# A matmul with batch normalization: one more raw block and one more y buffer

## The chip, the cores and the metric

The kernel runs on one core of a Trainium2 chip. The metric is the time of one execution on the device, in microseconds (us). Three runs of the kernel before gave 206.24, 206.34 and 206.34 us; their median is 206.34 us. A separate execution was profiled.

## The reference

```python
y = np.matmul(x, weight)                      # x: 16 x 512 x 1024, weight: 1024 x 768, float32
mean = np.mean(y, axis=(0, 1), keepdims=True)
var = np.var(y, axis=(0, 1), keepdims=True)
y_norm = (y - mean) / np.sqrt(var + eps)
return (gamma * y_norm + beta).astype(np.float32)
```

There are 8192 rows (16 x 512) and 768 columns. Each column needs its mean and variance over all rows before its first output can be written.

## The kernel before, in words

**Tiling.** The 768 columns are six tiles of 128, called nt = 0 to 5. The 8192 rows are 16 chunks c of 512. x and weight are loaded and cast to bf16 by GpSimd's DMA queue (L386, L402); VectorE turns x so that the depth of 1024 stands on the partitions (L424, L431). x stays on the chip, turned, to the end.

**Tiles 0 and 1** are computed while x arrives, with rows on the partitions (L506). ScalarE squares each block (L655), VectorE adds it to `sum1` (L658), and VectorE or GpSimd adds the squares to `sum2` or `sum3` (L662). When the last chunk but two is in, `merge` (L791) and `more` (L796) fold the accumulators into one row of sums and one row of squares, in a tile of their own, `tot`; TensorE sums those over the partitions (L867). The last two chunks take another path (L810). The output is formed by `rows_out` (L926): a product on VectorE (L933), an addition on VectorE or GpSimd (L938), a store (L942).

**Tiles 2 to 5** are computed with columns on the partitions (L571), chunk after chunk: tile 2 over chunks 4 to 15 from about 104 us on, then tiles 3, 4 and 5 (chunks 0 to 3 of all were done early, L571 too). Statistics are taken on VectorE (L707), or for tile 2 on ScalarE (L716, L720), and the block is kept in bf16 (L711) in a y buffer of 1024 rows, that is, two chunks. `finish_tasks` (L964) makes scale and shift of a tile. Then each y buffer has to be scaled, turned back to rows, widened to float32 and stored, in one of these ways:

- `col_block` (L1187) in mode `xact`, tiles 2 and 3: a scaling on ScalarE (tile 2) or VectorE (tile 3, L1022), a DMA turn on SyncE's queue (L1216), a conversion on ScalarE (L1228), a store (L1198).
- `col_block` in mode `pe`, tile 4: a scaling on VectorE, a turn on TensorE between the products of tile 5 (L1040), a conversion on ScalarE (L1206), a store.
- a **raw block**: the unscaled buffer is turned by DMA ahead of time, into another y buffer (`raw_turn`, L1095, its DMA is L1102). Once scale and shift are known, `raw_spread` (L1123) lays them out along the rows (L1137 to L1154, with seven small copies on GpSimd or ScalarE, L1141, and a copy into PSUM, L1154), and `raw_block` (L1162) makes a product on VectorE (L1170), an addition on GpSimd (L1174) and a store (L1178). `RAW` lists the blocks by their first chunk: chunks 0 and 2 of tile 2, chunk 0 of tile 3, chunks 0, 2 and 4 of tile 4.
- `held_block` (L1236): the last block of tile 4, held back and stored (L1251) while the statistics of tile 5 are made.

Tile 5 comes last: its statistics end with L1304, scale and shift with L1320, and then its blocks are scaled (L1344), turned on TensorE (L1040), converted (L1357) and stored (L1360). In the text below tile nt = 3 is "the fourth tile" and nt = 4 "the fifth".

**Plain chunks.** For some chunks ScalarE or VectorE copies the turned x into a plain layout `x_pl` (`part_chunk`, L524, L543); for the chunks 12 to 15 this is done just before tile 4, by whichever engine the planner picks.

**The order of the work** is made while the program is built: every step is a `Task` with a priority, the engines that could do it with an estimated duration, and what it waits for. `arrange` (L122) takes the tasks one by one, by engine free times, buffers (`Pool`, `Space`), the DMA lanes (`Wires`) and priority, and so writes a fixed order for each engine. A change to one number can move instructions of other steps.

**Buffers.** Product results have 8 PSUM banks. There are `YB` = 28 y buffers of 2 KB per partition, shared by kept blocks, turned raw blocks and one plain chunk part; and a ring of 24 KB per partition (`RING`, `Space`) for loaded x, later for turned blocks (2 KB) and float32 output blocks (4 KB). SyncE's queue (SPq) issues all stores and turns in order; each waits for the landing of the eighth one before it at the latest.

**Gamma and beta** are loaded by `load_affine` (L406), twelve transfers of 128 values on SyncE's queue, one pair per tile.

Of the kernel before, what the change touches and what calls it, by code (L numbers as in the profile page):

```python
# [227 lines left out]
def kernel(  # L228
# [9 lines left out]
    nc = tc.nc  # L238
    f32 = mybir.dt.float32
# [8 lines left out]
    P = 128  # L248
    NT = N // P
# [3 lines left out]
    C = M // CH  # L253
# [9 lines left out]
    EARLY = 4  # L263
    SHORT = 2
    GA = 2
    NA = GA * P
    GY = 2
    PAD = 50
    HELD = 1
    ASTAT = {2:tuple(range(4,16))}  # L270
    RC = C - 2
    XT, YB, SQ = C - EARLY, 28, 3
    ADDED = (0,6,16,28,40)
    PARTED, LATE, SINGLE = (4,5,7,8,9,10), (12,13,14,15), (2,3,6)
    MODE = {2:'xact',3:'xact',4:('pe',)*8}
    MODE = {nt: m if isinstance(m, tuple) else (m,) * (C // GY) for nt, m in MODE.items()}
    RAW, RAWADD, RAWDUE = {2:(0,2),3:(0,),4:(0,2,4)}, {2:'POOL',3:'POOL',4:'POOL'}, {2:14.0,3:8.0,4:8.0}
    RING = 3 * CH // 32 * KQ // 2
    ENG = {"ACT": nc.scalar, "DVE": nc.vector, "POOL": nc.gpsimd, "SP": nc.sync}

# [3 lines left out]
    singles = ctx.enter_context(tc.tile_pool(name="singles", bufs=1))  # L284
# [7 lines left out]
    def seq(bi):  # L292

        ins = bi.ins
        prev = last.get(ins.engine)
        if prev is not None:
            tc.add_manual_dep(
                ins, prev,
                mybir.DependencyInfo(mybir.DependencyClass.NoSync, mybir.DependencyReason.DATA),
                reason="order",  # L300
            )
        last[ins.engine] = ins.name
        return bi

    gamma_sb = singles.tile([P, NT], f32)
# [10 lines left out]
    ones = singles.tile([P, 1], f32)  # L316
    seq(nc.vector.memset(ones, 1.0 / (RC * CH)))
    ident32 = singles.tile([P, P], f32)
    sum1 = singles.tile([P, 2 * NA], f32)
    sum2 = singles.tile([P, 2 * NA], f32)  # L320
    sum3 = singles.tile([P, 2 * NA], f32)
    for acc in (sum1, sum2, sum3):
        seq(nc.vector.memset(acc, 0.0))
    tot = singles.tile([P, 2, NA], f32)
    stats = singles.tile([P, (NT - GA) * C + PAD, 6], f32)
    fin = singles.tile([P, 9 + 6 * len(PIECES)], f32)
    psums = {nt: singles.tile([P, 2, C], f32, name=f"psums{nt}") for nt in ASTAT}
    sums = {nt: singles.tile([P, 4 + 6 * C], f32, name=f"sums{nt}") for nt in ASTAT}
    for nt in ASTAT:
        seq(nc.vector.memset(sums[nt][:, 1:2], float(len(ASTAT[nt]) * CH)))  # L330
    msq = singles.tile([P, GA], f32)
# [74 lines left out]
    def load_affine(eng):  # L406
        seq(nc.vector.memset(gamma_sb, 0.0))
        seq(nc.vector.memset(beta_sb, 0.0))
        for nt in range(NT):
            seq(nc.sync.dma_start(gamma_sb[:, nt:nt + 1], gamma[nt * P:(nt + 1) * P, None]))  # L410
            seq(nc.sync.dma_start(beta_sb[:, nt:nt + 1], beta[nt * P:(nt + 1) * P, None]))

    def turn_x(xslot, slot, m0, t0, jw0, jw1, new, rows=QR):
# [28 lines left out]
    t = 1.0  # L442
    affine = None
    for kind, n, *n1 in order:
# [12 lines left out]
        if m0 == M // 2:  # L457
            affine_loads = affine = task(t, {"SP": (5.0, 7.0)}, load_affine, [x_ready[m0 // CH - 3, 0, JW]])
# [235 lines left out]
    def stats_of(nt):  # L694
        return stats[:, (nt - GA) * C:(nt - GA + 1) * C]
# [3 lines left out]
    def col_stats(nt, c, slot, t):  # L699
        now = clock[0]  # L700

        def bn(eng):
            dst = fin[:, 3:9] if (nt, c) == (NT - 1, C - 2) else stats_of(nt)[:, c, :]
            if nt in ASTAT:
                i = 4 + 6 * [j for j in range(C) if j not in ASTAT[nt]].index(c)
                dst = sums[nt][:, i:i + 6]
# [81 lines left out]
    def merge(i):  # L788
        def emit(eng):
            acc = (sum1, sum2)[i]  # L790
            seq(ENG[eng].tensor_add(tot[:, i], acc[:, 0:NA], acc[:, NA:2 * NA]))  # L791
        return emit

    def more(h):
        def emit(eng):
            seq(nc.gpsimd.tensor_add(tot[:, 1], tot[:, 1], sum3[:, h * NA:(h + 1) * NA]))  # L796
        return emit

    ga_half = {}
# [61 lines left out]
    def sums_rows(eng):  # L861
        tot_ps = psum.tile([P, CH], f32, tag="b")
        aff["tot"] = tot_ps
        for i in range(2):
            for a in range(GA):
                j = i * GA + a
                seq(nc.tensor.matmul(  # L867
                    tot_ps[:, j:j + 1], tot[:, i, a * P:(a + 1) * P], ones,
                    start=True, stop=True, skip_group_check=True,
                ))  # L870

# [40 lines left out]

    U = S - 30.0
    s1 = task(U, pe(0.9), sums_rows, merges, takes=[tot_slot])
    se = task(U, dve(0.8), sums_entry, [s1], True, uses=[tot_slot])
    ag = [task(U, dve(0.25), aggregate_rows(a), [se] + [h[0] for k, h in ga_half.items() if k[0] == a]) for a in range(GA)]
# [347 lines left out]
    for nt in range(GA, NT - 1):  # L1264
# [14 lines left out]
        for i in range(C // GY):  # L1279
            if (nt, GY * i) in raw:  # L1280
                raw_block(nt, GY * i, start + STEP[nt] * i + RAWDUE[nt])
                continue
            if nt == NT - 2 and C // GY - HELD <= i:
                held.append((nt, GY * i, f))
# [4 lines left out]
    nt = NT - 1  # L1289
# [45 lines left out]
    for c, r0, rows in ends:  # L1335
        due = E + 2.0 + 0.6 * c
        n = max(rows // CH, 1)
# [70 lines left out]
```

## Time and profile before

| what | time |
|---|---|
| median of three runs | 206.34 us |
| the profiled execution, its own time | 206.02 us |
| its span, first to last instruction | 204.2 us |
| TensorE busy | 189.3 us (93%) |
| VectorE busy | 159.5 us (78%) |
| ScalarE busy | 145.9 us (71%) |
| GpSimd busy | 124.1 us (61%) |
| last product of tile 5 ends | 186.4 us |
| scale and shift of tile 5 ready (L1320) | 187.9 us |
| first store of tile 5 issued | 189.1 us |
| last conversion of tile 5 ends | 196.4 us |

The profile is that of one execution. A row of its timeline begins with the start and the duration in us, then the engine, the line of the kernel, the operation and its operands, how many were merged, and in brackets how long the engine stood idle before and what ended that. Rows of grouped instructions give the count, the busy time, the mean duration in ns and the idle time before them. PE is TensorE, PEld its weight loads, DVE is VectorE, ACT is ScalarE, POOL is GpSimd, SP is SyncE, and a q behind a name means that engine's instruction queue.

### The profile page before, as it was taken

What the parts mean: (1) busy time and instruction counts of PE and PEld (TensorE: products, weight loads), DVE (VectorE), ACT (ScalarE), POOL (GpSimd) and SP (SyncE); (2) the same over time, 40 slices, a digit from 0 to 9 for tenths busy, and PEclk for the clock granted to TensorE, in tenths of its full rate; (3) what the DMA queues carried; (4) which work ended last, traced back from release to release, by engine and by line L of the source; (5) the groups of instructions that cost most, each with busy time, mean ns of one, the idle gap of its engine ahead of it and who ended that gap; (6) DMA issues with size and microseconds to landing.
All of it is one profiled execution on the core that took longest, in us unless ns stands there. A gap on an engine that the chain in (4) does not pass through costs nothing.

```text
span 204.2 us, 3511 instructions
## 1 busy us (share of the span) xinstructions
PE 189.3 (93%) x1210; PEld 114.7 (56%) x1210; DVE 159.5 (78%) x250; ACT 145.9 (71%) x260; POOL 124.1 (61%) x150
## 2 busy tenths in 40 slices
PE   7979999999999999999999999999999999996900
PEld 3458555656588888777875444444444445544600
DVE  4031879999999999969989998977999788657800
ACT  2001461369989999998979766999997969946940
POOL 7876954877499989996404999389512312840000
PEclk9999999999999999999999999999999999999965
DMA  4999999999999999999698898999999999999997
GB/s 75 163 200 195 193 196 196 196 197 196 190 193 196 197 199 193 196 197 195 104 157 219 312 340 313 269 303 313 301 295 227 336 303 306 347 344 311 311 347 225
DMA packets 98578, 48.74 MB, mean 239 GB/s; under 512 B 24320, under 2 KB 98048, under 8 KB 98560
## 3 DMA queue, kind: packets, MB, share of 16 engines
q0 software_dynamic: 34624, 18.36, 65.2%
q1 hardware_dynamic: 63936, 30.16, 54.7%
q8 instruction: 9, 0.15, 0.3%
q14 instruction: 9, 0.07, 0.1%
HBM read 36.71 MB, written 25.17 MB: 303 GB/s over the span
## 4 chain that ended last, share of the span: by engine, by line
PE 79%; DMA 9%; ACT 3%; POOL 2%; DVE 1%; issue 1%; ACTq 0%; DVEq 0%; POOLq 0%
PE y_ps L571 51%; PE y_ps L506 21%; DMA w_sb<-in_weight_dram 6%; PE y_ps L810 4%; ACT o_sb L1357 3%; DMA ring<-in_x_dram 3%; PE o_ps L1040 1%; POOL ring L402 1%; PE y_ps L749 1%; POOL w_sb L386 1%; DVE xT_sb L431 1%; PE a_ps L899 1%; PE o_ps L1070 0%; ACTq L1403 0%; PE tot_ps L867 0%
## 5 line engine op out<-in xcount | busy, mean ns | idle before, releaser
L571 PEld LDWEIGHTS <-w_sb 128*128 128x128 bf16 x520 | 50.3, 97 | 57.6
L571 PE MATMUL y_ps<-xT_sb,w_sb 128*128 128x512 bf16 (+1 forms) x272 | 59.3, 371 | 0.0
L571 PE MATMUL y_ps<-x_pl,w_sb 128*128 128x512 bf16 x248 | 57.4, 379 | 0.0
L402 POOL DMA_DIRECT2D ring<-in_x_dram x76 | 47.4, 630 | 13.2 <-DVE xT_sb L424 5.0
L506 PE MATMUL y_ps<-w_sb,xT_sb 128*128 128x256 bf16 x448 | 50.5, 273 | 1.5 <-DMA ring<-in_x_dram 1.3
L506 PEld LDWEIGHTS <-xT_sb 128*128 128x128 bf16 x448 | 43.6, 98 | 9.0 <-DVE xT_sb L431 2.4
L431 DVE STREAM_TRANSPOSE xT_sb<-ring 128x1024 f32<-128x1024 f32 (+1 forms) x29 | 31.2, 1111 | 13.4 <-DMA ring<-in_x_dram 13.3
L707 DVE BATCH_NORM_STATS2 stats<-y_ps 128x6 f32<-128x512 f32 x46 | 30.9, 686 | 7.1 <-PE y_ps L571 6.7
L711 ACT CAST y_sb<-y_ps 128x512 bf16<-128x512 f32 x51 | 29.0, 594 | 9.3 <-DVE stats L707 5.6
L543 ACT COPY x_pl<-xT_sb 128x1024 bf16<-128x1024 bf16 x32 | 32.8, 1061 | 1.7 <-DVE xT_sb L431 1.7
L938 POOL TENSOR_TENSOR ring<-ring,sum 128x1024 f32<-128x1024 f32 (+1 forms) x11 | 23.7, 2181 | 15.0 <-ACT y_ps L720 10.9
L655 ACT ACTIVATE sq_sb<-y_ps 128x512 f32<-128x512 f32 x28 | 16.5, 612 | 17.2 <-PE y_ps L506 16.3
L662 POOL TENSOR_TENSOR sum<-sum,sq_sb 128x512 f32<-128x512 f32 x20 | 25.6, 1280 | 3.8 <-ACT sq_sb L655 2.7
L658 DVE TENSOR_TENSOR sum<-y_ps,sum 128x512 f32<-128x512 f32 x28 | 18.9, 675 | 6.4 <-ACT sq_sb L655 5.3
L668 ACT CAST y_sb<-y_ps 128x512 bf16<-128x512 f32 x28 | 16.0, 601 | 7.5 <-DVE sum L658 7.4
L1174 POOL TENSOR_TENSOR ring<-ring,sum 128x1024 f32<-128x1024 f32 x6 | 14.8, 2462 | 10.4 <-issue 9.0
L933 DVE TENSOR_TENSOR ring<-y_sb,a_ps 128x1024 f32<-128x1024 bf16 (+1 forms) x16 | 16.7, 1077 | 0.0
L1228 ACT CAST ring<-ring 128x1024 f32<-128x1024 bf16 x13 | 13.8, 1062 | 1.4 <-DMA ring<-y_sb 1.4
L1040 PE MATMUL o_ps<-ident,y_sb 128*128 128x128 bf16 x104 | 13.1, 221 | 1.6 <-DVE y_sb L1344 1.5
L424 DVE STREAM_TRANSPOSE xT_sb<-ring 128x2048 bf16<-128x2048 bf16 x6 | 13.5, 2289 | 0.2 <-DMA ring<-in_x_dram 0.2
L1141 POOL COPY sum<-sum 32x256 f32<-32x256 f32 (+1 forms) x17 | 5.7, 336 | 12.9 <-DVE sum L1138 6.5
L587 PE MATMUL idle_ps<-idle_sb 128*128 128x512 f32 x18 | 9.7, 690 | 1.5 <-DVE idle_sb L315 1.5
(104 smaller groups left out, 154.0 us busy)
## 6 DMA issues: line engine op xcount, KB each, us to landing
out_dram<-ring SPq DMA_DIRECT2D x37, 512.0 KB, 3.4
ring<-in_x_dram POOLq DMA_DIRECT2D x52, 256.0 KB, 8.7
out_dram<-o_sb SPq DMA_DIRECT2D x6, 512.0 KB, 4.7
ring<-in_x_dram POOLq DMA_DIRECT2D x16, 128.0 KB, 6.0
w_sb<-in_weight_dram POOLq DMA_DIRECT2D x8, 192.0 KB, 6.1
out_dram<-ring SPq DMA_DIRECT2D x6, 256.0 KB, 3.0
ring<-in_x_dram POOLq DMA_DIRECT2D x4, 192.0 KB, 7.7
out_dram<-o_sb SPq DMA_DIRECT2D x3, 256.0 KB, 2.5
```

The lines of the kernel that those rows point to most:

```text
L402: bi = seq(nc.gpsimd.dma_start(x_bf[32 * i:32 * i + 32], src[:, :, KQ * i:KQ * (i + 1)]))
L431: seq(nc.vector.transpose(dst, src[:, :, jw0:jw1]))
L506: seq(nc.tensor.matmul(y_ps[:, s], x_of(c, jw, e, t * P, (t + 1) * P), w_sb[:, jw, e, 0:NA], start=(s == 0 and jw == 0 and e == 0), stop=( ...
L543: seq(nc.scalar.copy(dst, pairs) if eng == "ACT" else ENG[eng].tensor_copy(dst, pairs))
L571: seq(nc.tensor.matmul(y_ps, w_sb[:, jw, e, nt * P:(nt + 1) * P], moving(c, jw, e, q0 * QR, q1 * QR, parted), start=(jw == 0 and e == 0 an ...
L655: seq(nc.scalar.activation(sq_sb[:, 0:n], slot.tile[:, 0:n], AF.Square))
L658: seq(nc.vector.tensor_add(sum1, slot.tile[:, 0:n], sum1))
L662: seq(ENG[eng].tensor_add(acc, acc, state["sq"][:, 0:n]))
L707: seq(nc.vector.bn_stats(dst, slot.tile))
L711: seq(nc.scalar.copy(y(nt, c), slot.tile))
L933: seq(nc.vector.tensor_mul(slot.o, y_row[c].y[:, s0:s1], aff[0][:, None, :].to_broadcast([P, n, NA])))
L938: seq(ENG[eng].tensor_add(slot.o, slot.o, row[:, None, :].to_broadcast([P, n, NA])))
```

## The change

Four things, in one diff:

- `merge` and `more` write the totals into the first halves of `sum1` and `sum2`, and TensorE reads them there; the tile `tot` (2 KB per partition) is gone.
- `YB` is 29 instead of 28, which takes 2 KB per partition.
- Tile 3 has a second raw block, chunks 2 and 3. Its turn (L1102) is asked for with the other early ones, before tile 2's products; its scaling, its turn on the way out (L1216) and its conversion (L1228) are replaced by L1170 and L1174.
- `load_affine` loads gamma's first two columns with one transfer of 256 values, and loads all of gamma before beta: eleven transfers.

```diff
     HELD = 1
+    PAIRED = 1
...
-    XT, YB, SQ = C - EARLY, 28, 3
+    XT, YB, SQ = C - EARLY, 29, 3
...
-    RAW, RAWADD, RAWDUE = {2:(0,2),3:(0,),4:(0,2,4)}, {2:'POOL',3:'POOL',4:'POOL'}, {2:14.0,3:8.0,4:8.0}
+    RAW, RAWADD, RAWDUE = {2:(0,2),3:(0,2),4:(0,2,4)}, {2:'POOL',3:'POOL',4:'POOL'}, {2:14.0,3:8.0,4:8.0}
...
-    tot = singles.tile([P, 2, NA], f32)
...
+        for nt in range(0, NT, 2):
+            n = 2 if nt < 2 * PAIRED else 1
+            for i in range(nt, nt + 2, n):
+                seq(nc.sync.dma_start(gamma_sb[:, i:i + n], gamma[i * P:(i + n) * P].rearrange("(t p) -> p t", p=P)))
         for nt in range(NT):
-            seq(nc.sync.dma_start(gamma_sb[:, nt:nt + 1], gamma[nt * P:(nt + 1) * P, None]))
             seq(nc.sync.dma_start(beta_sb[:, nt:nt + 1], beta[nt * P:(nt + 1) * P, None]))
...
-            seq(ENG[eng].tensor_add(tot[:, i], acc[:, 0:NA], acc[:, NA:2 * NA]))
+            seq(ENG[eng].tensor_add(acc[:, 0:NA], acc[:, 0:NA], acc[:, NA:2 * NA]))
...
-            seq(nc.gpsimd.tensor_add(tot[:, 1], tot[:, 1], sum3[:, h * NA:(h + 1) * NA]))
+            seq(nc.gpsimd.tensor_add(sum2[:, 0:NA], sum2[:, 0:NA], sum3[:, h * NA:(h + 1) * NA]))
...
-                    tot_ps[:, j:j + 1], tot[:, i, a * P:(a + 1) * P], ones,
+                    tot_ps[:, j:j + 1], (sum1, sum2)[i][:, a * P:(a + 1) * P], ones,
```

In the built order TensorE's instructions are the same, one for one. VectorE, ScalarE, GpSimd and SyncE keep their order up to the output of tile 3, but for the lines of the diff and the sixth early turn behind the five. From there to the start of tile 4's output some instructions change places: the scalings of tile 3, the plain copies of chunks 14 and 15 (of the latter's four, ScalarE makes three and VectorE one, where it was one and three), and the conversions and stores around the new raw block.

## The prediction

> **What bounds the kernel now.** I read the page first, then who waits for whom on TensorE, the windows of the last third, and the issue views of SyncE's queue (SPq).
>
> ```profile
> span 204.2 us, 3511 instructions
> PE 189.3 (93%) x1210; PEld 114.7 (56%) x1210; DVE 159.5 (78%) x250; ACT 145.9 (71%) x260; POOL 124.1 (61%) x150
> ```
> ```profile
> PE idle_ps L587 <- DVE idle_sb L315: 1.5, 1, 1.5
> PE y_ps L506 <- DMA ring<-in_x_dram: 1.3, 1, 1.3
> PE o_ps L1040 <- DVE y_sb L1344: 1.5, 1, 1.5
> ```
>
> These three rows are the whole list of TensorE's waits: two at the start of the program and one behind its last product, none in the middle. So nothing that the change frees between the first and the last product can move TensorE forward; it can only make TensorE wait. What is left is the tail.
>
> ```profile
> 168.00:172.50 4.50, 4.50 (x33) 2.43 (x31) 3.70 (x10) 4.09 (x9) 1.35 (x3) 1.00 1.20 296
> 172.50:187.00 14.50, 14.32 (x94) 7.88 (x92) 9.54 (x16) 10.12 (x16) 7.09 (x3) 1.00 1.15 345
> 187.00:191.00 4.00, 2.62 (x31) 1.72 (x32) 3.73 (x14) 3.49 (x9) 0.00 (x0) 1.00 0.88 264
> 191.00:202.00 11.00, 2.84 (x36) 1.89 (x34) 2.39 (x8) 5.42 (x7) 0.00 (x0) 0.72 1.14 344
> ```
> ```profile
> 171.54 4.47 SPq L1198 DMA_DIRECT2D out_dram<-ring  x4
> ...
> 183.29 1.40 SPq L1178 DMA_DIRECT2D out_dram<-ring  x1
> ```
> ```profile
> out_dram<-ring SPq DMA_DIRECT2D x1, 512.0 KB, 3.0
> ...
> out_dram<-ring SPq DMA_DIRECT2D x1, 512.0 KB, 6.0
> ...
> out_dram<-o_sb SPq DMA_DIRECT2D x1, 512.0 KB, 3.2
> ...
> out_dram<-ring SPq DMA_DIRECT2D x1, 512.0 KB, 2.8
> ```
>
> The columns are the stretch, the busy time of TensorE, its weight loads, VectorE, ScalarE and GpSimd, the granted clock, the DMA share and GB/s. From 172.5 us to 187 and again from 191 to 202 the stores run at 345 and 344 GB/s: the wires are full. A 512 KB store (524,288 B) at 345 GB/s takes 1.52 us. The four landing rows are those of single stores: issued at 171.54 us, it lands after 3.0 us; the last old one, issued at 183.29, after 6.0 (at 189.3, behind a queue); one of the last tile, issued at 191.4, after 3.2; and, for the scale, one at 120.3 that finds the wires almost empty, after 2.8. So the queue is last short at the store of 171.54 and backs up from there to the end. **The end is set by when that store is issued, and by the bytes behind it.** The mean of 264 GB/s from 187 to 191 is the one slack spot, while the last tile's statistics are made.
>
> ```profile
> 169.86 0.59 ACT L711 CAST y_sb<-y_ps 128x512 bf16<-128x512 f32 x1
> 170.47 1.04 ACT L1228 CAST ring<-ring 128x1024 f32<-128x1024 bf16 x1
> 171.43 0.38 ACT L1154 COPY a_ps<-sum 128x256 f32<-128x256 f32 x1
> ```
>
> That store waits for the ScalarE conversion that ends at 171.51 us, which stands on ScalarE behind a keep (L711) that follows the products and the statistics of the last tile, TensorE's pace again.
>
> **The change part by part.** Sums are made against the profiled execution's 206.02 us (span 204.2 and 1.8 around it); the median of the three runs shown, 206.34, lies 0.32 above, and the forecast is given on that scale.
>
> *Totals in the accumulators.* One addition on VectorE (L791), three on GpSimd (L791, twice L796) and TensorE's sums (L867) keep their count and size; only where the result goes is new: 0.0. Writing in place is what L662 does throughout, so I see no price; were there one of 0.1 us an instruction, TensorE would have other products to do around its sums.
>
> *Gamma's pair.* Twelve small transfers become eleven, gammas first.
>
> ```profile
> 48.15 0.36 SPq L410 DMA_DIRECT2D gamma_sb<-in_gamma_dram  x1
> ...
> 99.52 8.68 SPq L1102 DMA_TRANSPOSE r_sb<-y_sb  x5
> 108.85 0.41 SPq L942 DMA_DIRECT2D out_dram<-ring  x1
> ```
>
> One issue of 0.36 us is saved in a queue that then has nothing until 99.5 us: 0.0, and it stays so if the paired transfer takes twice as long.
>
> *The sixth early turn.* The turn of the fourth tile's second block moves from the loaded stretch to this one: five turns from 99.52 to 108.20 become six. At (108.20 - 99.52) / 5 = 1.74 us each the sixth would end at 109.9 and hold back the first store (108.85) by 1.1; in the built order the later turns wait for landings one turn further back than before, so I take 0.3. Either way it meets wires that are far from full and no wait of TensorE: 0.0, bounds 0 and 1.1, covered by the stores' own room until the fourth tile.
>
> *The 29th buffer* is taken by the turned block from there until its product is formed near 158 us; what waits for a freed buffer waits for a neighbour instead. 0.0.
>
> *The second raw block itself.* For one block: a VectorE scaling, a turn among the stores and a ScalarE conversion go; a VectorE product and a GpSimd addition come.
>
> ```profile
> L1228 ACT CAST ring<-ring 128x1024 f32<-128x1024 bf16 x13 | 13.8, 1062 | 1.4 <-DMA ring<-y_sb 1.4
> L1022 DVE TENSOR_SCALAR y_sb<-y_sb,scale,shift 128x1024 bf16<-128x1024 bf16 x12 | 6.4, 541 | 0.1
> L1170 DVE TENSOR_TENSOR ring<-r_sb,a_ps 128x1024 f32<-128x1024 bf16 x6 | 7.3, 1217 | 2.7 <-DMA out_dram<-ring 2.7
> L1174 POOL TENSOR_TENSOR ring<-ring,sum 128x1024 f32<-128x1024 f32 x6 | 14.8, 2462 | 10.4 <-issue 9.0 <-DVE ring L1170 1.2
> L543 DVE COPY x_pl<-xT_sb 128x1024 bf16<-128x1024 bf16 x8 | 5.2, 680 | 0.0
> L543 ACT COPY x_pl<-xT_sb 128x1024 bf16<-128x1024 bf16 x32 | 32.8, 1061 | 1.7 <-DVE xT_sb L431 1.7
> ```
>
> In the built order of the changed kernel the planner also hands two copies of the last plain x chunk from VectorE to ScalarE. VectorE: -0.54 + 1.22 - 2 x 0.68 = -0.68 us. ScalarE: -1.06 + 2 x 1.06 = +1.06. GpSimd: +2.46. What has to hold is the date at which the fifth tile's statistics are complete:
>
> ```profile
> 154.73 0.38 ACT L1154 COPY a_ps<-sum 128x256 f32<-128x256 f32 x1 [0.20 <-POOL sum L1141]
> 158.00 1.04 ACT L1228 CAST ring<-ring 128x1024 f32<-128x1024 bf16 x1 [0.94 <-DMA ring<-y_sb]
> ...
> 164.47 0.59 ACT L711 CAST y_sb<-y_ps 128x512 bf16<-128x512 f32 x1 [0.71 <-DVE stats L707]
> ```
> ```profile
> 160.26 1.22 DVE L1170 TENSOR_TENSOR ring<-r_sb,a_ps 128x1024 f32<-128x1024 bf16 x1 [1.00 <-DMA out_dram<-ring]
> 163.74 0.70 DVE L707 BATCH_NORM_STATS2 stats<-y_ps 128x6 f32<-128x512 f32 x1 [0.60 <-PE y_ps L571]
> 167.80 0.53 DVE L1022 TENSOR_SCALAR y_sb<-y_sb,scale,shift 128x1024 bf16<-128x1024 bf16 x1
> ```
> ```profile
> 168.93 0.22 PE L1040 MATMUL o_ps<-ident,y_sb 128*128 128x128 bf16 x1
> ```
> ```profile
> 83.60 1.73 PE y_ps L571 x8
> ```
>
> ScalarE idles at least 0.94 + 0.71 = 1.65 us between 154.7 and 164.5; 1.06 of it is taken, 0.59 stays. VectorE: the first raw product can start when the coefficients are in PSUM, near 154.8, and ends at 156.0. The second waits for ring space whose store is issued at 151.43 and lands 5.6 us later:
>
> ```profile
> out_dram<-ring SPq DMA_DIRECT2D x1, 512.0 KB, 5.6
> ```
>
> at 157.1, so it ends at 158.3. GpSimd's additions: 156.0 to 158.5 and 158.5 to 161.0. Behind the second product stand four statistics (0.70 each, the row at 163.74), three scalings (0.54 each) and one more statistic. The fourth needs products that end two blocks before those of 163.74, at 1.73 us a block (the row of the chain) at 160.3, which is over by then: 158.3 + 4 x 0.70 = 161.1, + 3 x 0.54 = 162.7, + 0.70 = 163.4. The next statistic starts at 163.74, when its products end: **0.3 us of room**. Behind it the first scaled block of the fifth tile ends at 168.33 and TensorE takes it at 168.93 (the turn of L1040): 0.6 more. Nothing moves: 0.0 for TensorE.
>
> *The tail.* The ten ring stores from 171.54 on are ten again, in the same order of kinds; the first still follows the conversion that starts at 170.47. What goes is the turn that filled the wires just before (296 GB/s from 168 to 172.5; in the built order one turn fewer stands before that store), so this store may land after 2.8 us instead of 3.0: -0.2 at best, 0 at worst. I take -0.1, since the store itself waits for the same conversion in both. The coefficients' copy (171.43) now stands behind one more conversion, 0.95 us later, and the fifth tile's first raw store, which follows the four of 171.54 at 176.0, comes at most that much later, at 177.0; those four take the wires until 172.5 + 4 x 1.52 = 178.6, so it waits anyway.
>
> Sum: 206.02 - 0.1 = 205.9 in the profile's terms, 206.34 - 0.1 = **206.2 us**.
>
> **The rivals.** *GpSimd's pair of additions pushes the fifth tile's statistics (slower).* The scalings behind them share a resource with GpSimd:
>
> ```profile
> 130.94 4.68 POOL L938 TENSOR_TENSOR ring<-ring,sum 128x1024 f32<-128x1024 f32 x2 [3.58 <-DVE ring L933]
> ```
> ```profile
> 134.94 0.71 DVE L1137 COPY sum<-scale 128x32 f32<-128x32 f32 x1
> 135.57 0.17 DVE L1137 COPY sum<-shift 128x32 f32<-128x32 f32 x1
> ```
>
> A copy that takes 0.17 us took 0.71 and ended at 135.65, where GpSimd's addition ended (135.62). If the first addition waits out a scaling (+0.5), both take 2.75 as the longest of the six did instead of 2.46 (+0.6),
>
> ```profile
> L1174 POOL TENSOR_TENSOR ring<-ring,sum x6: 2355/2388/2746, 140.8 to 179.4; 128x1024 f32<-128x1024 f32 x6
> ```
>
> and the ring's store lands 1 us later, the second addition ends at 161.0 + 2.1 = 163.1, and three scalings and a statistic (2.3 us) follow: 165.4 where 163.4 was counted. Past 0.3 + 0.6 = 0.9 us of room this costs 1.1 us, as TensorE waits and every store of the run with it: 207.3. It decides from a second addition that ends after 163.74 + 0.6 - 2.3 = 162.0. For it speaks the thin room; against it, the worked end of 161.0, a whole microsecond short of it.
>
> The Trainium skill, SBUF — State Buffer, section Who interferes with whom, says that VectorE's copy and scaling in a two-port mode and a GpSimd instruction exclude each other, whoever starts first holding the ports for the whole instruction. The 0.71 agrees; by that rule alone the scalings would start at the addition's end, 161.0, which is the date worked out above.
>
> *The wires start earlier (faster).* If one old store fewer were left at 187 us, the last tile's stores would find empty wires: 2.8 instead of 3.2 for the one issued at 191.4, so 0.4 is the most, 205.9, since its issue is bound to the last statistics. Against it: ten stores remain, and their first waits for the same keep.
>
> *It doesn't do what it says:* the raw store waits in SPq's order behind others, the turn's place is filled by nothing, and the time is 206.3.
>
> **How the numbers follow.** Forecast 0.55, the change without effect 0.14 (both within 0.2%, 0.41 us, which is about what a measurement of this kernel can tell from no change), the additions' rival 0.23, the wires' rival 0.08. The last lies at the bound and is counted as faster; of the additions' rival 0.01 is too small to leave the middle. Faster 0.08, same 0.55 + 0.14 + 0.01 = 0.70, slower 0.22. The range goes from 205.8 (the best tail) to 207.0, which takes in most of the additions' rival, 207.3 at its full price.
>
> **What would show it.** Right: TensorE's list of waits has the same three rows; the fifth tile's statistics are complete at 165; the conversion before the last run of stores starts at 170.5; 345 GB/s from 172.5 on; GpSimd has two L1174 in a row, the second over before 162.0. Wrong: a wait of TensorE for VectorE or ScalarE between 160 and 180, or a window after 172.5 below 340 GB/s ahead of the last statistics; or a run of ten stores that begins well before 171.5.

## The result and the profile after

The changed kernel takes 206.03 us (median of 20 runs, 205.32 to 206.49), the kernel before 206.42 us (20 runs, 205.75 to 207.44). The medians lie 0.39 us apart; the ratio on record, which is not simply that of the medians, is 0.9975, 95% interval 0.9963 to 0.9987: 0.25% faster, or 0.52 us (0.27 to 0.76). The forecast was 206.2 us, 0.1 less than before: sign and range held, and 0.43 us of the gain is something that the prediction did not have. The profiled execution of after took 205.96 us, the one of before 206.02, so the two traces show nearly the same span; what differs between them has to be read place by place.

The page of after, its span and its first row, and TensorE's whole list of waits:

```profile
span 204.2 us, 3509 instructions
...
PE 191.0 (94%) x1210; PEld 116.3 (57%) x1210; DVE 158.7 (78%) x248; ACT 146.6 (72%) x261; POOL 126.1 (62%) x151
```
```profile
PE o_ps L1043 <- DVE y_sb L1347: 1.5, 1, 1.5
PE idle_ps L590 <- DVE idle_sb L316: 1.5, 1, 1.5
PE y_ps L509 <- DMA ring<-in_x_dram: 0.6, 1, 0.6
```

The same three waits as before (most lines stand 3 lower in the file): nothing in the middle of the program. The stretches of the tail, columns as in the prediction, and the two steps that set its start, on ScalarE and in SyncE's queue:

```profile
168.00:172.50 4.50, 4.50 (x32) 2.37 (x31) 3.66 (x10) 3.89 (x8) 1.35 (x3) 1.00 0.96 245
172.50:187.00 14.50, 14.50 (x96) 8.02 (x94) 9.63 (x15) 9.94 (x17) 7.03 (x3) 1.00 1.13 339
187.00:191.00 4.00, 2.43 (x28) 1.56 (x27) 3.69 (x14) 3.48 (x9) 0.00 (x0) 0.95 0.89 268
191.00:202.00 11.00, 3.76 (x41) 3.58 (x38) 2.68 (x9) 5.71 (x7) 0.00 (x0) 0.66 1.13 341
```
```profile
170.75 1.99 ACT L1231 CAST ring<-ring 128x1024 f32<-128x1024 bf16 x2
```
```profile
171.82 3.96 SPq L1201 DMA_DIRECT2D out_dram<-ring  x4
...
183.67 1.39 SPq L1181 DMA_DIRECT2D out_dram<-ring  x1
```

From 86 us on, up to its last product, TensorE stands 0.28 us later in this execution than in that of before, and the conversion (170.75 against 170.47) and the first store (171.82 against 171.54) stand later by just that. One turn less goes through ahead of 172.5, the last one before the stores is issued at 168.27 instead of 169.10 (245 GB/s against 296), and then the wires are full as before: the 339 GB/s come from the window, which begins 0.28 us too early for this execution; from 172.78 to 187.28 it is 345. Up to here nothing is gained, and yet the span is not 0.28 longer.

**Where the gain lies: behind the last landing.** SyncE's list of waits at the end of the program, of before and of after (what it waited for, us in total, times, longest):

```profile
SPq L1403 <- DMA out_dram<-o_sb: 3.0, 1, 3.0
```
```profile
SPq L1406 <- DMA out_dram<-o_sb: 3.3, 3, 1.5
```

Before waits once, 3.0 us; after waits three times, for three stores in turn. Those are SyncE's last semaphore instructions, and the trace has a record of each, which the views above do not print:

```
before  202.91 to 202.94   the wait that the last landing (202.90) ends
        202.98, 203.04, 203.10, 203.16, 203.22, 203.28, 203.34   seven more waits
        203.41 drain ... 204.2 end
after   199.63 ... 199.87  waits that find their store landed
        201.00, 202.53     two that are ended by the stores before the last
        203.27 to 203.30   the wait that the last landing (203.26) ends
        203.34 drain ... 204.2 end
```

SyncE's transfers take eight semaphores in turn, as the trace shows for each of them (that is why each transfer waits for the eighth before it), and at the end of the program SyncE waits for the eight in a fixed order, the same in all the kernels here. Before has 89 transfers on that queue; 89 is one more than a multiple of eight, so the last store has the first semaphore, and seven waits of 0.06 us follow its landing. After has 88: the last store has the last semaphore, and the seven waits ahead of it were over before it landed. From the last landing to the end of the span it is 1.35 us before and 0.92 after: **0.43 us**, which one small transfer less brings. The experiments test that.

### The profile page after: what moved, and what is told of

The parts are those of the page before. It is cut to its first block, busy times and chain, and to the rows that moved or that the text cites. A ratio compares the mean times of both kernels' runs of the same rounds, so it can differ in the third digit from the quotient of the medians.

```text
span 204.2 us, 3509 instructions
## 1 busy us (share of the span) xinstructions
PE 191.0 (94%) x1210; PEld 116.3 (57%) x1210; DVE 158.7 (78%) x248; ACT 146.6 (72%) x261; POOL 126.1 (62%) x151
## 4 chain that ended last, share of the span: by engine, by line
PE 86%; ACT 3%; DMA 3%; POOL 2%; issue 1%; ACTq 0%; DVE 0%; POOLq 0%
PE y_ps L574 54%; PE y_ps L509 24%; PE y_ps L813 4%; ACT o_sb L1360 3%; DMA ring<-in_x_dram 3%; PE o_ps L1043 1%; POOL ring L402 1%; POOL w_sb L386 1%; PE y_ps L752 1%; PE a_ps L902 1%; PE o_ps L1073 0%; ACTq L1406 0%; PE idle_ps L590 0%; PE tot_ps L870 0%; ACT ring L1251 0%
## 5 line engine op out<-in xcount | busy, mean ns | idle before, releaser
L546 ACT COPY x_pl<-xT_sb 128x1024 bf16<-128x1024 bf16 x34 | 34.8, 1063 | 1.7 <-DVE xT_sb L434 1.7
L1177 POOL TENSOR_TENSOR ring<-ring,sum 128x1024 f32<-128x1024 f32 x7 | 17.1, 2469 | 4.5 <-issue 2.7
L1043 PE MATMUL o_ps<-ident,y_sb 128*128 128x128 bf16 x104 | 13.7, 249 | 1.6 <-DVE y_sb L1347 1.5
L1231 ACT CAST ring<-ring 128x1024 f32<-128x1024 bf16 x12 | 12.6, 1060 | 0.6 <-DMA ring<-y_sb 0.5
L590 PE MATMUL idle_ps<-idle_sb 128*128 128x512 f32 x18 | 10.5, 741 | 1.5 <-DVE idle_sb L316 1.5
```

The lines of the kernel that those rows point to most:

```text
L546: seq(nc.scalar.copy(dst, pairs) if eng == "ACT" else ENG[eng].tensor_copy(dst, pairs))
L1177: seq(ENG[eng].tensor_add(slot.o, slot.o, row[:, None, :].to_broadcast([P, n, P])))
```

## The experiments

In each run the kernel before was timed on the same chip; ratios are against those runs.

**Which part of the change.** Four kernels: gamma alone, the totals and the 29th buffer alone, the change without gamma, the change again.

`e1_gamma`: before, with the change's part on gamma (eleven transfers; the ends of long lines are left out)

```diff
+    PAIRED = 1
...
+        for nt in range(0, NT, 2):
+            n = 2 if nt < 2 * PAIRED else 1
+            for i in range(nt, nt + 2, n):
+                seq(nc.sync.dma_start(gamma_sb[:, i:i + n], ...
         for nt in range(NT):
-            seq(nc.sync.dma_start(gamma_sb[:, nt:nt + 1], ...
             seq(nc.sync.dma_start(beta_sb[:, nt:nt + 1], ...
```

> The kernel before with gamma's part alone: eleven transfers, gammas ahead of betas, the first two in one. Four theories of the ratio 0.9975 (about 0.5 us). Raw (the turn, the conversion and the scaling that leave the loaded stretch free the wires ahead of the last stores): 1.000 here. Gamma (the small transfers lie beside the loads of x, and one fewer or another order lets x arrive earlier): 0.9975 here. Totals (in place, with every later tile at another address): 1.000 here. Chance (nothing is gained, the 20 runs of each fell so): 1.000 here, with an interval of about 0.0012 to either side.

Measured: 205.95 us against 206.59; 0.9967 (0.9953 to 0.9980). The gamma part alone gives the whole gain.

`e2_totals`: before, with

```diff
-    XT, YB, SQ = C - EARLY, 28, 3
+    XT, YB, SQ = C - EARLY, 29, 3
...
-    tot = singles.tile([P, 2, NA], f32)
... (totals go to sum1 and sum2, as in the change)
```

> The kernel before with the totals in the accumulators and 29 y buffers, no second raw block, gamma as before. Every engine has the order of before. Raw: 1.000. Gamma: 1.000. Totals: 0.9975, and TensorE's sums or the first products of the third tile earlier by 0.5 us. Chance: 1.000.

Measured: 206.69 against 206.59; 1.0002 (0.9986 to 1.0018). The totals in place and the 29th buffer are free.

`e3_no_gamma`: the changed kernel with gamma's part taken back, that is, the lines of `e1_gamma` the other way round (twelve transfers).

> The changed kernel with gamma's loads as before, so totals, 29 buffers and the second raw block. Raw: 0.9975. Gamma: 1.000. Totals: 0.9975. Chance: 1.000.

Measured: 206.47 against 206.59; 0.9999 (0.9985 to 1.0013). The second raw block neither gains nor costs.

`e4_again`: the changed kernel, unaltered.

> The changed kernel once more, unaltered, for the spread. Raw, Gamma and Totals: 0.9975 with an interval that lies below 1. Chance: an interval that holds 1.

Measured: 205.90 against 206.59; 0.9977 (0.9959 to 0.9994). Raw, Totals and Chance fall; Gamma stands, and the question becomes what about gamma: its order, its pair, or the number.

**Order, pair or number.** `e5_order`: before, with

```diff
+    PAIRED = 0
... (the other lines as in e1_gamma: gammas ahead of betas, twelve transfers)
```

> The kernel before with the gammas loaded ahead of the betas, but none in a pair: twelve small transfers as before. Two theories of gamma's gain. Lane: SyncE's transfers take eight semaphores in turn, and at the end SyncE waits for the eight in a fixed order, some 0.06 us each; with 89 transfers the last store has the first of them and seven more waits follow its landing (from the last wait that holds to the end 0.43 us more), with 88 it has the last of them. Load: the order or the pairing of the small transfers lets x through better beside them. Lane: ratio 1.000, and SyncE waits at its end once, for one transfer, with the span's end 1.3 us behind the last landing. Load: 0.9975 if the order does it, 1.000 if the pair does it.

Measured: 206.55 against 206.38; 1.0002 (0.9986 to 1.0018), one wait at the end, 1.35 us from the last landing to the end. The order alone does nothing: it is the pair, or the number of transfers that goes with it. SyncE's waits for the last stores in this kernel:

```profile
SPq L1407 <- DMA out_dram<-o_sb: 3.1, 1, 3.1
```

The next three add transfers, so that the number changes without a pair. `e6_seven` and `e7_three` are before, `e8_one` is the changed kernel, each with

```diff
+    extra = singles.tile([P, n], f32)                      (n = 7, 3, 1; behind `touched`)
+    for i in range(n):
+        seq(nc.sync.dma_start(extra[:, i:i + 1], beta[i % NT * P:(i % NT + 1) * P, None]))
```

> The kernel before with seven more small transfers behind the twelve, whose values nothing reads: 96 on SyncE's queue instead of 89. Lane: 96 is a multiple of eight, the last store has the last semaphore again, 0.43 us less: 0.998, in spite of more work; SyncE waits at its end three times, and the span ends 0.9 us behind the last landing. Load: seven more transfers beside the loads of x, 1.000 or slower.

> The kernel before with three more small transfers: 92. Lane: the last store has the fourth semaphore, four waits follow instead of seven, 0.18 us less than before: 0.999, and 1.1 us from the last landing to the span's end. Load: 1.000 or slower.

> The changed kernel, pair and order of gamma and all, with one more small transfer, whose values nothing reads: 89 again. Lane: the gain is gone, 1.000 against the kernel before, and 1.3 us from the last landing to the span's end. Load: the gain stays, 0.9975.

Measured: 208.53, 209.08 and 208.96 against 206.38; 1.0098 (1.0075 to 1.0121), 1.0122 (1.0101 to 1.0143), 1.0120 (1.0096 to 1.0145). All three missed Lane's times by over 2 us; Load's "1.000 or slower" covers the first two by its letter, but not the third, for which it said 0.9975. Their ends were as Lane said (from the last landing to the end of the span 0.93, 1.16 and 1.35 us with 96, 92 and 89 transfers), but the last 512 KB stores landed some 1.8 us apart instead of 1.51. The new tile takes 32 bytes per partition in the built program, and every tile behind it, the output buffers `o_sb` among them, had moved by 32 bytes. So the experiment had changed two things. The next three part them.

`e10_seven_inplace` (before) and `e11_one_inplace` (changed kernel), n = 7 and 1; the one instruction that wrote `warm` now writes its column 0:

```diff
-    warm = singles.tile([P, 1], f32)
+    warm = singles.tile([P, 8], f32)                       (the same 32 bytes)
...
+    for i in range(n):
+        seq(nc.sync.dma_start(warm[:, i + 1:i + 2], beta[i % NT * P:(i % NT + 1) * P, None]))
```

> The kernel before with the seven more small transfers once more (96 instead of 89, their values read by nothing), this time into columns of a tile that is there already, so that no other tile gets another address. Lane: 0.43 us less than before, 0.998; SyncE waits at its end three times and the span ends 0.9 us behind the last landing. Load: 1.000 or slower, with the last nine stores at 345 GB/s. If the transfers themselves made the earlier run with seven more slower, 1.010 again.

Measured: 206.26 against 206.49; 0.9990 (0.9972 to 1.0008), that is -0.2 us (-0.6 to +0.2). The end is Lane's: three waits, 0.93 us from the last landing to the end. The time is on Lane's side of 1, but the interval holds 1 too, so the trace carries this one, not the clock.

> The changed kernel with one more small transfer (89 again), into a column of a tile that is there already. Lane: 1.000 against the kernel before, 1.3 us from the last landing to the span's end. Load: 0.9975. If one more transfer costs by itself, 1.012 again.

Measured: 206.63 against 206.49; 1.0002 (0.9989 to 1.0015), 1.35 us to the end. The changed kernel with its pair, its order, its raw block, and one transfer that does nothing: the gain is gone. With that, Load by order or by pairing falls. Load by number (one transfer fewer beside the loads of x) does not, since this kernel has twelve small transfers behind one another again; it is taken up below, behind the table of the ends. SyncE's waits for the last stores, e10 and then e11:

```profile
SPq L1405 <- DMA out_dram<-o_sb: 3.1, 3, 1.5
```
```profile
SPq L1408 <- DMA out_dram<-o_sb: 3.0, 1, 3.0
```

`e12_pad`: before, with

```diff
     touched = singles.tile([P, 2, TOUCH], f32)
+    pad = singles.tile([P, 1], f32)
+    seq(nc.vector.memset(pad, 0.0))
```

> The kernel before with a tile of 32 bytes per partition ahead of the output and y buffers, and no transfer more (a memset of 128x1 is all that is added). Address: the 32 bytes by which the later tiles move slow the last stores from 1.51 to some 1.83 us for 512 KB, as in the three runs with a new tile: 1.010 to 1.012. If the transfers were to blame there: 1.000.

Measured: 208.91 against 206.49; 1.0115 (1.0095 to 1.0136). Two stretches of this kernel, columns as above:

```profile
172.50:187.00 14.50, 14.47 (x96) 7.91 (x92) 9.76 (x15) 10.12 (x16) 7.12 (x3) 1.00 1.15 341
...
191.00:202.00 11.00, 3.34 (x43) 3.16 (x40) 2.57 (x8) 5.93 (x7) 0.00 (x0) 0.66 0.96 281
```

The stores out of the ring, which lies ahead of the new tile and has not moved, run at 341 GB/s, much as in before (345); those out of `o_sb` at 281 instead of 344. Six 512 KB stores land in 11.10 us (193.61 to 204.71) instead of 9.07 (193.08 to 202.15): 1.85 each, not 1.51. No transfer was added here, so the transfers were not to blame in the three runs with a new tile.

**The rival of the prediction.** `e9_twice`: the changed kernel with

```diff
+            for _ in range(2 if (nt, c) == (3, 0) else 1):
                 seq(ENG[eng].tensor_add(slot.o, slot.o, row[:, None, :].to_broadcast([P, n, P])))
```

> The changed kernel with GpSimd's first addition of the fourth tile's pair made twice (so that block has the shift twice), which puts the second one's end from 161.1 us to 163.5 on the scale of the changed kernel's profile. The prediction's rival (the fifth tile's three scalings wait for GpSimd): they start at 163.5, the tile's last statistic ends 1.6 us later than at 164.7, 0.6 of it is TensorE's room, so 1.0 us on every later step: 207.0 us, 1.003 against the kernel before, and a wait of TensorE for VectorE of 1.0 us. If the scalings run beside the addition: nothing but one store is later, 0.9975.

Measured: 207.17 against 206.49; 1.0035 (1.0020 to 1.0049). GpSimd, VectorE, TensorE and SyncE's queue in this kernel; all of it stood 0.50 us later than after's trace when it came here:

```profile
156.68 7.32 POOL L1178 TENSOR_TENSOR ring<-ring,sum 128x1024 f32<-128x1024 f32 x3 [1.81 <-issue]
```
```profile
161.06 0.70 DVE L710 BATCH_NORM_STATS2 stats<-y_ps 128x6 f32<-128x512 f32 x1 [1.03 <-PE y_ps L574]
161.68 3.51 DVE L1025 TENSOR_SCALAR y_sb<-y_sb,scale,shift 128x1024 bf16<-128x1024 bf16 x3
165.11 1.28 DVE L710 BATCH_NORM_STATS2 stats<-y_ps 128x6 f32<-128x512 f32 x2
```
```profile
170.15 0.23 PE L1043 MATMUL o_ps<-ident,y_sb 128*128 128x128 bf16 x1 [0.28 <-DVE y_sb L1025]
```
```profile
173.30 3.96 SPq L1202 DMA_DIRECT2D out_dram<-ring  x4
```

The three scalings take 3.51 us where they take 1.45 in after. It is the first of them that is held up: it takes 2.60 us (161.68 to 164.28) beside the third addition (161.62 to 163.99), and the other two, behind it, take 0.53 each as usual. The Trainium skill, SBUF — State Buffer, section Who interferes with whom, says that one of the two blocks the other for its whole instruction; by that rule, the trace agrees. TensorE waits 0.28 us for VectorE, as in no other of these kernels between the loads and its last product, and falls back by 0.45 in all; the last run of stores begins 0.98 later and the last landing comes 1.19 later (both beside the 0.50). The rival was priced at 1.0: the run's delay is 0.98, the landing's 1.19. It is real, and in the changed kernel it did not happen because the second addition ended early enough (161.08 there, and the scalings began at 161.18).

**All ends side by side.** From the last landing to the end of the span, by the number of transfers on SyncE's queue:

| transfers | waits behind the last landing | kernels | us |
|---|---|---|---|
| 89 | 7 | before, e2, e3, e5, e8, e11, e12 | 1.35 each |
| 92 | 4 | e7 | 1.16 |
| 88, 96 | 0 | after, e1, e4, e9; e6, e10 | 0.92 to 0.93 |

(1.35 - 0.92) / 7 = 0.061 us a wait; with 4 it would be 1.17.

Nothing of the kind is found in the loads. From its first product to 110 us TensorE took 0.06 to 0.53 us longer than in before in the four profiled executions with 88 transfers, and 0.02 to 0.41 longer in the other six with 89. So Load by number finds no support in these traces, one for each kernel.

## Why the prediction was right or wrong, point by point

*TensorE can't move forward.* Held for what the change frees on the other engines: its list of waits has the same rows, and behind 87 us nothing in the changed kernel moves it any more. Before that its places move with the loads of x, which differ from one execution to the next (see the last section).

*The end is set by the store of 171.54 and the bytes behind it.* Held as far as the last landing: store and conversion moved with TensorE, by the same 0.28. But the end of the span is not the last landing, and the prediction took all behind it as fixed.

*Totals in the accumulators, 0.0; the 29th buffer, 0.0.* Held: 1.0002 (0.9986 to 1.0018).

*Gamma's pair, 0.0.* This is the step that failed: "One issue of 0.36 us is saved in a queue that then has nothing until 99.5 us: 0.0". The issue is indeed covered. What the sum left out is that a transfer is also a turn in the round of semaphores, and so sets where the last store stands in the row of waits at the end: -0.43. Both halves of it were at hand: the wait of 3.0 us for one store, with 1.35 us from there to the end, in the trace of before, and the round of eight, by which each transfer waits for the eighth before it.

*The sixth early turn, 0.3 taken for the first store, 0.0 for the end.* The store was not held at all. SyncE's queue in after:

```profile
100.19 8.10 SPq L1105 DMA_TRANSPOSE r_sb<-y_sb  x6
109.14 0.77 SPq L945 DMA_DIRECT2D out_dram<-ring  x1
```

Six turns take 8.10 us where five took 8.68, so 1.74 us was no price of a turn. In after the six are issued one behind the other, 1.35 us each. In before the 8.68 held a wait: the third turn landed only after 4.56 us, at 106.91, and the fifth was issued at 106.96. The store came at 109.14, 0.29 behind before's, which is TensorE's shift.

*The second raw block, 0.0.* Held: 0.9999 (0.9985 to 1.0013) without gamma. The groups of after:

```profile
L1177 POOL TENSOR_TENSOR ring<-ring,sum 128x1024 f32<-128x1024 f32 x7 | 17.1, 2469 | 4.5 <-issue 2.7 <-DMA out_dram<-ring 1.8
L1231 ACT CAST ring<-ring 128x1024 f32<-128x1024 bf16 x12 | 12.6, 1060 | 0.6 <-DMA ring<-y_sb 0.5
L1173 DVE TENSOR_TENSOR ring<-r_sb,a_ps 128x1024 f32<-128x1024 bf16 x7 | 8.5, 1214 | 1.4 <-DMA out_dram<-ring 0.8 <-ACT a_ps L1157 0.6
```

The counts are the forecast's, 7, 12 and 7. The chain on VectorE and GpSimd, in after:

```profile
156.43 1.21 DVE L1173 TENSOR_TENSOR ring<-r_sb,a_ps 128x1024 f32<-128x1024 bf16 x1
157.56 1.98 DVE L710 BATCH_NORM_STATS2 stats<-y_ps 128x6 f32<-128x512 f32 x3
160.56 0.70 DVE L710 BATCH_NORM_STATS2 stats<-y_ps 128x6 f32<-128x512 f32 x1 [1.03 <-PE y_ps L574]
161.18 1.45 DVE L1025 TENSOR_SCALAR y_sb<-y_sb,scale,shift 128x1024 bf16<-128x1024 bf16 x3
162.54 0.70 DVE L710 BATCH_NORM_STATS2 stats<-y_ps 128x6 f32<-128x512 f32 x1
164.02 0.70 DVE L710 BATCH_NORM_STATS2 stats<-y_ps 128x6 f32<-128x512 f32 x1 [0.78 <-PE y_ps L574]
```
```profile
156.19 4.89 POOL L1177 TENSOR_TENSOR ring<-ring,sum 128x1024 f32<-128x1024 f32 x2 [1.81 <-DMA out_dram<-ring]
```

The second product ended at 157.6, not 158.3: the store that it waited for landed after 3.7 us here, not 5.6. The additions ended at 161.08 (forecast 161.0), and the chain had 0.78 us of room (forecast 0.3): VectorE idles that long for TensorE's products before the last statistic.

*The tail, -0.1.* Not seen. The first store landed after 2.95 us instead of 3.02, but from one of TensorE's turns of the last tile (at 190.28 in before) to the last landing it was 12.69 us against 12.62, and between 12.61 and 12.94 in the other kernels whose addresses and additions were left alone. The term is below what the executions differ by. So the forecast's sign, which rests on this -0.1 alone, came true for another reason: that is luck.

*The rivals.* The additions' rival did not occur, and `e9_twice` showed its mechanism and about its price. The wires' rival, which alone stood for "faster" (0.08), did not occur: 268 GB/s from 187 to 191 us against 264, and 261 from 187.28 to 191.28. "The change without effect" would have been right for the part that the change is mostly made of. The gain fell outside all the cases, small enough to stay in the range. Of the signs that the prediction named, those for a right course came: the three waits, the two additions over at 161.08 (before 162.0), the last statistic of the fifth tile over at 164.72, the conversion at 170.75. The wires are a special case: 339 GB/s from 172.5 to 187 lies under the 340 that the prediction named as a sign of being wrong, but only because the window was not moved with the execution (345 when it is). None of these signs looked at the end of the program, where the gain is.

*What remains.* The interval of the gain, 0.27 to 0.76 us, holds the 0.43; what is left of the 0.52 is not told from zero.

## What to carry to other kernels

The end of a program is a stage like any other: take apart the time from the last landing to the end of the span, and see whether the last store's semaphore is the last that is waited for; adding or dropping one transfer on the queue ahead of it moves it, here by up to 0.43 us. When a part of a change saves something in an idle queue, ask also what counts along with it (a round of buffers or semaphores, an address). And an experiment that adds a tile moves all tiles behind it: put test data into room that is there already.

## What the runs showed of the hardware that was not expected

- **A wait that is long satisfied still takes time.** Each of SyncE's last waits takes 0.06 us (202.98, 203.04, 203.10, ...), also when its transfer landed long ago.
- **Stores depend on the start address in SBUF.** In the built programs `o_sb` begins at byte 66,560 of a partition in before, a multiple of 512, at 64,512 in after, also one, and at 66,592 in `e12_pad`, a multiple of 32 only: 344 GB/s became 281. Which multiple is enough was not tried. The Trainium skill, DMA: Bandwidth & Descriptors, section How a descriptor splits into AXI transactions, says that a piece which does not begin at a multiple of 256 bytes is cut at the boundaries of 256 and costs transactions and beats more. For rows of 512 bytes begun 32 late that is 17 beats in three transactions for 16 in two; by the beats alone 1.51 us would be 1.60 (an estimate from that page). The direction agrees; the measured 1.85 is more, and decides. The 512-byte packets themselves last hardly longer (27.8 ns on average in `e12_pad` from 193.5 to 201.5 us, 27.0 in before); what grew is the distance from one to the next, and the DMA share fell from 1.14 to 0.96.
- **The first loads differ from one execution to the next.** TensorE's first products began between 11.6 and 13.0 us in the profiled executions of all these kernels, a spread that is more than the gain explained here. The profiled execution of `e4_again` was the longest of its twelve, 207.55 us; its wait for x, against 0.6 in the one of after and 1.3 in that of before (206.02 us):

```profile
PE y_ps L509 <- DMA ring<-in_x_dram: 1.5, 1, 1.5
```

  How much of the spread of the runs this makes was not shown.
- Between 78 and 87 us TensorE fell back by 0.3 to 0.7 us against before in the four profiled executions with 88 transfers, and by 0.3 in `e6_seven` (96) and `e7_three` (92), but by less than 0.1 in those with 89 and in `e10_seven_inplace` (96); at 25 us the six had won 0.2 to 0.3. The number of transfers alone does not sort them. The cause is open.
